# A hybrid decoder step in float32: when the down stage casts its operands, and in which order its weights

## The chip, the cores and the metric

The kernel runs on one core of one Trainium2 chip. The metric is the time of one execution in microseconds, the median of the runs shown. TensorE multiplies matrices out of SBUF into PSUM; VectorE, ScalarE and GpSimd do the element-wise work; SP issues most of the DMAs. In the profile's rows they are PE (PEld is its weight load), DVE, ACT, POOL and SP (SPq its queue).

## The reference

One layer of a decoder, for 1024 prompt tokens and 32 sampled ones (1056 in all), in float32. Attention and a state-space mixer come first; the stage of this change is the second half of the feed-forward block:

```python
def post_mixer(h, mix, p, w_out, ln1_g, ln1_b, w_up, w_down, w_pe, w_pg, b_pg, ln2_g, ln2_b):
    h1 = layer_norm(ALPHA * h + mix @ w_out, ln1_g, ln1_b)
    ff = jnp.square(jax.nn.relu(h1 @ w_up)) @ w_down
    e = jax.nn.sigmoid(h1 @ w_pg + b_pg) * (p @ w_pe)
    return layer_norm(ALPHA * h1 + ff + e, ln2_g, ln2_b)
```

`w_up` is 1024 x 4096, `w_down` 4096 x 1024.

## The kernel before

**Split numbers.** Every matmul operand is held as two tiles of the matmul type: a high part, made by a cast on ScalarE (`S.copy`), and a low part, the float32 value minus the high part. A product is then three matmuls, high x high, high x low and low x high.

**Seven products for eight.** The matrix product with `w_down` is done in 2 x 2 blocks by a Strassen-Winograd scheme: seven products per block. Four of the seven take sums of weight blocks as weights (`s1` to `s4`, made by `sums` on GpSimd: s1, then s2 from s1, s3, and s4 from s2), three take a weight block itself (high part `whi`, low part `wlo`). A sum gets its high part from ScalarE (`ring`, tile `a`) and its low part on GpSimd. The operands of the seven products were made by the up stage and lie in DRAM (`gd`).

**Groups and units.** The loop over `gr` (0 to 6, seven groups) walks over the inner dimension, the loop over `m` (0 to 3, four units) over the output columns. A unit is seven products in the order of `PO` (P1, P2, P3, P5, P7, P6, P4; products 0 to 6 in what follows), each of 12 matmuls of 128 x 264 into one PSUM tile `pd`; there are four such banks, taken in turn. Each product is evacuated into the accumulator `pacc` of its `m`: an addition on VectorE, or in group 0 for four of the seven a copy on ScalarE (L1599). Products 2, 3, 4 and 5 use the sums s4, s1, s3 and s2. The up stage runs before group 0, and an eighth group with the layer norm (the tail) after group 6. After units 0 and 1 of group 6, `combine` adds up a finished accumulator, half on VectorE and half on GpSimd; for units 2 and 3 the tail does it.

**Operands.** Seven operands per group, common to its four units, are loaded one group ahead. `put` is a generator: its first step issues the load (L1427), its second casts the high part on ScalarE and subtracts the low part on VectorE (L1429 and a subtraction in the helper at L82). Two are loaded in unit 0, two in unit 1, one in unit 2, and the last two, for products 5 and 6, in unit 3. There are 12 operand slots; a slot comes free when the last product on its old operand is done.

**Weights.** `dload` fetches the raw weights of the next unit in four DMAs (L1443), with two buffers. `split` makes `whi` and `wlo` (VectorE), `dsums` the four sums and their parts; the four `a` tiles are a ring.

**What sets the order.** A scheduler orders the instructions of each engine from the program and its own estimate of times, and may move an instruction over others; each engine then runs its own list strictly in order. `tc.issue_after(...)` holds what stands under it behind a given instruction; `newest(engine)` is the last one written so far for an engine. So a list is neither the program's order nor free of it.

Of the kernel before, what the change touches and what calls it, by code (L numbers as in the profile page):

```python
# [69 lines left out]
def fox_s5_step(tc, a, o):  # L70
    nc = tc.nc
    V, S, G, PE, SY = nc.vector, nc.scalar, nc.gpsimd, nc.tensor, nc.sync
# [8 lines left out]
    def tt(e, out, x, y, op):  # L81
        e.tensor_tensor(out, x, y, op=op)  # L82
# [27 lines left out]
    def bank2(name, tag="w"):  # L110
        return cur["pool"].tile([128, 2, 512], F32, tag=tag, name=name, bufs=cur["bufs"][tag])
# [44 lines left out]
    def split(x, hi, lo, e=V):  # L156
        S.copy(hi, x)  # L157
        tt(e, lo, x, f(hi), SUB)
# [6 lines left out]
    def newest(engine):  # L165
        return [i for i in nc.cur_bb.bb.instructions if i.engine == engine][-1]
# [136 lines left out]
    with ExitStack() as st1:  # L303
# [127 lines left out]
        for l in range(L):  # L431
            j = L - 1 - l
# [296 lines left out]
        for u in range(3):  # L729
            ps = flip()  # L730
            n = 4 if u < 2 else 1
# [550 lines left out]
    for n, i in enumerate(order):  # L1282
# [3 lines left out]
        if 0 < n < 8:  # L1286
            x = order[n + 1]
# [37 lines left out]
    with ExitStack() as st1:  # L1325
# [24 lines left out]
        for m in range(8):  # L1350
            w = load_w(a["w_pg"][0][:, 128 * m:128 * m + 128]) if m > 1 else wg[m]
            if m < 4:
                x, y = [pp.tile([128, 2, HN], F32, tag=f"x{j}", name="x") for j in range(2)]
# [33 lines left out]
    def sums(p, x11, x12, x21, x22, n):  # L1387
        s1, s2, s3, s4 = (p.tile([128, 4 if p is up_ else n, 128], F32, tag=f"s{j}", name="s")[:, 0:n] for j in range(4))
        tt(G, s1, x21, x22, ADD)
        tt(G, s2, s1, x11, SUB)  # L1390
        tt(G, s3, x11, x21, SUB)
        tt(G, s4, x12, s2, SUB)
        return s1, s2, s3, s4

    def ring(p, x, n, bufs, e=V):
        x_ = p.tile([128, 2, 4 if p is up_ else n, 128], F32R, tag="a", name="a", bufs=bufs)[:, :, 0:n]
        split(x, x_[:, 0], x_[:, 1], e)
        return x_[:, 0], x_[:, 1]
# [5 lines left out]
    def product(ps, w, x, n, start):  # L1404
        for k in range(n):
            for j, (wt, xt) in enumerate(((w[0], x[0]), (w[0], x[1]), (w[1], x[0]))):
                for p in range(2):
                    PE.matmul(ps[:, p, :PC], lhsT=wt[:, k], rhs=xt[:, k, p * PC:(p + 1) * PC],  # L1408
                              start=(start and k == 0 and j == 0), stop=(k == n - 1 and j == 2), skip_group_check=True)
# [10 lines left out]
    def xslot():  # L1420
        n = (6, 7, 0, 1, 8, 9, 2, 3, 10, 11, 4, 5)[gn[0] % 12]
        gn[0] += 1
        return dn.tile([128, 2, 2, HN], F32R, tag=f"x{n}", name="x")

    def put(gr, c):
        xx = xslot()
        SY.dma_start(out=f(xx[:, 1]), in_=gd[gr][:, c])  # L1427
        yield
        S.copy(xx[:, 0], f(xx[:, 1]))  # L1429
        tt(V, xx[:, 1], f(xx[:, 1]), f(xx[:, 0]), SUB)  # L1430
        yield xx[:, 0], xx[:, 1]
# [3 lines left out]
    def q(x, fh, dh):  # L1435
        return x.rearrange("p (f k h) c -> p f k h c", f=2, k=2)[:, fh, :, dh]

    def dload(gr, m):
        raw, hi, lo = wraw()
        for j, z in enumerate((2 * gr, 2 * gr + NP_)):  # L1440
            for dh in range(2):
                d0 = (4 * dh + m) * 128
                SY.dma_start(out=q(raw, j, dh),  # L1443
                             in_=a["w_down"][0][z * 128:z * 128 + 256, d0:d0 + 128].rearrange("(k p) c -> p k c", p=128))
        return raw, hi, lo

    def accload(m):
        for u in range(2):
            SY.dma_start(out=pacc[m][:, P2 + 2 * u:P4 + 2 * u], in_=accd[m + 4 * u].rearrange("p (a n) -> p a n", a=2))

    def dsums(p, w, bufs, ss=None):
        raw, hi, lo = w
        if ss is None:
            ss = sums(p, q(raw, 0, 0), q(raw, 1, 0), q(raw, 0, 1), q(raw, 1, 1), 2)
        s1, s2, s3, s4 = (ring(p, x, 2, bufs, G) for x in ss)
        x11, x12, x22 = ((q(hi, fh, dh), q(lo, fh, dh)) for fh, dh in ((0, 0), (1, 0), (1, 1)))
        return (P1, x11), (P2, x12), (P3, s4), (P5, s1), (P7, s3), (P6, s2), (P4, x22)

    with ExitStack() as st1:
        up_ = pool("up", stack=st1)  # L1460
        for i in range(NP_):
# [7 lines left out]
            s1, s2, s3, s4 = sums(up_, r0[:, 0:4], r0[:, 4:8], r1[:, 0:4], r1[:, 4:8], 4)  # L1469
            s2, s1, s3, s4, x22 = (ring(up_, x, 4, 5) for x in (s2, s1, s3, s4, r1[:, 4:8]))  # L1470
# [71 lines left out]
            with tc.manual_schedule(engines={mybir.EngineType.Activation, mybir.EngineType.DVE}):  # L1542
                for c in "wp4ps5p6ppppab":
                    if c == "p":
                        xs_[PO[len(xs_)]] = next(st.pop(0))
                    elif c == "w":
                        split(*w)
                        ss = sums(up_, *(q(w[0], fh, dh) for fh, dh in ((0, 0), (1, 0), (0, 1), (1, 1))), 2)
                    elif c == "s":
                        ws = dsums(up_, w, 5, ss)  # L1550
                    elif c == "a":
                        square(0)
                    elif c == "b":
                        tc.keep_in_program_order(square(1))
                    else:
                        evac(int(c))
# [9 lines left out]
    def combine(m):  # L1566
        x = pacc[m]
        for n, (o, z) in enumerate(((P6, P1), (P2, P1), (P3, P5), (P7, P6), (P3, P6), (P4, P7), (P8, P5), (P8, P7))):
            tt((V, G, G, V, V, V, G, G)[n], x[:, o], x[:, o], x[:, z], ADD)

    for gr in range(NG_ - 1):
        st = [put(gr + 1, c) for c in (range(7) if gr < NG_ - 2 else (0, 3, 1, 2))]
        nx = []
        for m in range(4):
            if gr or m:
                if gr == 0:
                    accload(m)
                split(*wn)
                ws = dsums(dw, wn, 4)
            if gr and m == 0:  # L1580
                with tc.issue_after(newest(mybir.EngineType.Activation)):
                    for j in (P6, P4):
                        xs_[j] = next(xs_[j])
            put_ = [st.pop(0) for _ in range(min((2, 2, 1, 0)[m], len(st)))]
            for x in put_:
                next(x)
            with ExitStack() as st1:
                if put_:
                    st1.enter_context(tc.issue_after(newest(mybir.EngineType.SP)))
                if gr or m:  # L1590
                    wn = dload(gr + m // 3, (m + 1) % 4)
                else:
                    wn = w1
            for n, (j, w) in enumerate(ws):
                ps = bank2("pd", "b")
                product(ps, w, xs_[j], 2, True)
                o = pacc[m][:, j].rearrange("p (a n) -> p a n", a=2)
                if gr == 0 and j < P2:
                    S.copy(o, ps[:, :, :PC])  # L1599
                else:  # L1600
                    tt(V, o, ps[:, :, :PC], o, ADD)
                if m == 3 and n < 2 and st:
                    nx.append(st.pop(0))
                    next(nx[-1])
                if n in (3, 5) and put_:
                    nx.append(next(put_.pop(0)))
            if gr == NG_ - 2 and m < 2:
                combine(m)
        xs_ = dict(zip(PO, nx)) if gr < NG_ - 2 else {1: nx[0:2], 0: nx[2:4]}
# [3 lines left out]
    for m in range(4):  # L1613
        raw, hi, lo = dload(NG_ - 1, m) if m else wn
        if m > 1:
            x = xslot().rearrange("p a k n -> p (a k n)")
# [4 lines left out]
    with ExitStack() as st1:  # L1621
# [6 lines left out]
        for c0, c1, ts_ in ((792, NT, (7, 8)), (HN, 792, (5, 6)), (256, HN, (2, 3, 4)), (0, 256, (0, 1))):  # L1628
# [15 lines left out]
            for n, m in enumerate(ms):  # L1644
                ps = bank("mml")[:, :c1 - c0]
                for fh in range(2):
                    w, x = ws[m % 4][m // 4][fh], xs_[th][fh]
# [93 lines left out]
```

## Time and profile before

| | us |
|---|---|
| median of 3 runs (1489.22 to 1490.48) | 1489.49 |
| the profiled execution | 1489.35 |
| its span, first to last instruction | 1487.6 |
| TensorE busy | 1394.8 (94%) |
| VectorE busy | 984.8 (66%) |
| GpSimd busy | 676.9 (46%) |
| ScalarE busy | 638.8 (43%) |
| down stage, first matmul on `pd` to first of the tail | 1086.70 to 1414.05 |

Busy shares are means over stages with different limits, so the stage has to be read by itself. Times in the rows are microseconds from the start of the span. A row of the windows has the stretch, its length, the busy time (and number of instructions) of PE, PEld, DVE, ACT and POOL, the granted clock of TensorE as a share of its full 2.4 GHz, the busy share of the DMA engines, and the GB/s they moved. The windows of the units are cut at the first matmul of every unit, each 84 matmuls after the last. A row of a timeline has start and length, engine, line, operation, the tile written and those read, their shapes and the number of instructions merged; in brackets the engine's idle time before it and what ended it. L82 is a helper's line, so there the tiles tell what is done: `x<-x` is the low part of an operand, `wlo` that of a weight block, `a<-s,a` that of a weight sum, `s<-` a sum, `pacc<-pd,pacc` an evacuation, `pacc<-pacc` an addition of `combine`.

### The profile page before, as it was taken

How to read it: one execution, taken by the hardware profiler on the slowest of the kernel's cores; microseconds unless marked ns; L12 is line 12 of the kernel's file. 1: busy time of each engine (PE TensorE's matmuls, PEld its weight loads, DVE VectorE, ACT ScalarE, POOL GpSimd, SP SyncE). 2: the span in 40 equal slices, each digit the busy share in tenths (PEclk: the TensorE clock that was granted, in tenths of full speed). 3: DMA queues.
4: the chain of work that ended last, by engine and by line, in shares of the span. 5: the costliest groups of instructions: out<-in, count | busy, mean ns of one | idle time of the engine just before them, and what ended most of it. 6: DMA issues, size and time to landing. Idle time of an engine off the chain costs nothing. (4 is left out here: it accounts for less than half of the span.)

```text
span 1487.6 us, 26536 instructions
## 1 busy us (share of the span) xinstructions
PE 1394.8 (94%) x10045; PEld 1274.6 (86%) x10045; DVE 984.8 (66%) x1591; ACT 638.8 (43%) x1188; POOL 676.9 (46%) x627
## 2 busy tenths in 40 slices
PE   6998999979999899999999999999989999999886
PEld 5787898977757657799999999999989999899886
DVE  8559599558867644678745555555366667777777
ACT  4423434446756523452324444444475324344112
POOL 4313011126666400048655334443267667676935
PEclk8999999989999999999999999999999999999998
DMA  7564355596765582232234443444394423444212
GB/s 274 180 128 103 96 145 148 176 245 162 188 175 143 164 244 61 77 90 81 91 100 160 159 145 120 140 153 160 110 349 145 144 89 101 159 151 140 69 35 99
DMA packets 205736, 211.89 MB, mean 142 GB/s; under 512 B 43592, under 2 KB 166088, under 8 KB 205608
## 3 DMA queue, kind: packets, MB, share of 16 engines
q1 hardware_dynamic: 197288, 178.02, 41.4%
q0 software_dynamic: 8320, 32.18, 5.6%
q8 instruction: 79, 1.29, 0.3%
q14 instruction: 49, 0.40, 0.1%
HBM read 143.59 MB, written 66.55 MB: 141 GB/s over the span
## 5 line engine op out<-in xcount | busy, mean ns | idle before, releaser
L1408 PE MATMUL pd<-x,a 128*128 128x264 f32 x1344 | 176.0, 289 | 19.4 <-POOL a L82 12.5
L1408 PEld LDWEIGHTS pd<-x,a 128*128 128x128 f32 x1344 | 169.9, 192 | 22.8 <-POOL a L82 14.2
L82 DVE TENSOR_TENSOR pacc<-pd,pacc 128x528 f32<-128x528 f32 x180 | 124.3, 701 | 79.9 <-PE pd L1408 78.7
L157 ACT CAST a<-s 128x256 fp32r<-128x256 f32 (+1 forms) x176 | 83.7, 483 | 189.8 <-PE pd L1408 109.1
L82 POOL TENSOR_TENSOR a<-s,a 128x256 fp32r<-128x256 f32 x112 | 114.2, 1025 | 92.4 <-ACT a L157 92.4
L1408 PE MATMUL pb<-th,a 128*128 128x264 f32 x768 | 132.3, 284 | 0.0
L82 POOL TENSOR_TENSOR pl<-pe,ph 128x512 fp32r<-128x512 f32 (+1 forms) x96 | 100.5, 1056 | 67.8 <-DVE ph L905 43.8
L82 DVE TENSOR_TENSOR wlo<-raw,whi 128x1024 fp32r<-128x1024 f32 x68 | 100.5, 1477 | 43.6 <-ACT whi L157 30.1
L1408 PE MATMUL pd<-x,whi 128*128 128x264 f32 x672 | 111.4, 288 | 9.0 <-DVE pacc L82 6.9
L82 POOL TENSOR_TENSOR s<-raw 128x256 f32<-128x256 f32 (+1 forms) x72 | 76.9, 1071 | 75.7 <-DVE a L82 64.1
L1408 PEld LDWEIGHTS pb<-th,a 128*128 128x128 f32 x768 | 109.2, 189 | 0.0
L1408 PEld LDWEIGHTS pd<-x,whi 128*128 128x128 f32 x672 | 95.0, 191 | 10.8 <-ACT a L157 5.8
L82 DVE TENSOR_TENSOR x<-x 128x1056 fp32r<-128x1056 f32 (+2 forms) x67 | 89.3, 1349 | 13.1 <-ACT x L1429 12.5
L183 PE MATMUL mmc<-hhi,whi 128*128 128x352 f32 x288 | 94.6, 329 | 0.0
L183 PE MATMUL mmc<-hhi,wlo 128*128 128x352 f32 x288 | 94.3, 328 | 0.0
L183 PE MATMUL mmc<-hlo,whi 128*128 128x352 f32 x288 | 93.8, 326 | 0.0
L82 POOL TENSOR_TENSOR rs<-rs,mh 128x1 f32<-128x1 f32 (+1 forms) x27 | 20.6, 770 | 160.1 <-DVE rs L86 157.8
L82 DVE TENSOR_TENSOR a<-s,a 128x512 fp32r<-128x512 f32 x64 | 48.1, 756 | 47.5 <-ACT a L157 43.3
L1408 PE MATMUL pb<-tl,a 128*128 128x264 f32 x384 | 78.0, 285 | 0.0
L157 ACT CAST whi<-raw 128x1024 fp32r<-128x1024 f32 x48 | 50.4, 1051 | 61.5 <-PE pa L1408 27.0
L882 ACT ACTIVATE row<-ss,nm 128x384 f32<-128x384 f32 (+4 forms) x96 | 55.6, 584 | 37.9 <-DVE nm L878 36.5
L1408 PE MATMUL pd<-x,wlo 128*128 128x264 f32 x336 | 69.2, 288 | 0.0
(471 smaller groups left out, 3948.4 us busy)
## 6 DMA issues: line engine op xcount, KB each, us to landing
x<-gd SPq DMA_DIRECT2D x53, 528.0 KB
raw<-in_w_up_dram SPq DMA_DIRECT2D x32, 512.0 KB
raw<-in_w_down_dram SPq DMA_DIRECT2D x128, 128.0 KB
gd<-e POOLq DMA_DIRECT2D x14, 1056.0 KB, 7.4
gd<-c POOLq DMA_DIRECT2D x14, 792.0 KB, 5.3
pg<-in_cache_k_dram SPq DMA_DIRECT2D x32, 256.0 KB
pg<-in_cache_v_dram SPq DMA_DIRECT2D x32, 256.0 KB
raw<-in_w_in_dram SPq DMA_DIRECT2D x12, 512.0 KB
```

The lines of the kernel that those rows point to most:

```text
L82: e.tensor_tensor(out, x, y, op=op)
L157: S.copy(hi, x)
L183: PE.matmul(out, lhsT=wt[:, k], rhs=xt[:, k, c0:c0 + n], start=(k == 0 and i == 0), stop=(k == nk - 1 and i == 2))
L882: S.activation(out=pr_[:, c * n:(c + 1) * n], in_=ps, func=AF.Exp, scale=-1.0, bias=nm[:, i:i + 1], accum_out=lsum[:, h, i + 4 * c:i + 4 * ...
L1408: PE.matmul(ps[:, p, :PC], lhsT=wt[:, k], rhs=xt[:, k, p * PC:(p + 1) * PC], start=(start and k == 0 and j == 0), stop=(k == n - 1 and j = ...
```

## The change

Two things are written in another order, and no instruction is added or taken out. First, `dsums` casts the sums in the order in which the products use them: s4, s1, s3, s2 (before: s1 to s4). Second, an operand that is loaded in unit m is cast in unit m + 1, right behind the weight casts of that unit (`due`, under `tc.issue_after` of the newest instruction on ScalarE). Before, its cast was written into unit m, after products 3 and 5, where nothing held it. For the last two operands of a group nothing changes in the code: they were cast behind the weight casts of unit 0 already.

```diff
         raw, hi, lo = w
         if ss is None:
             ss = sums(p, q(raw, 0, 0), q(raw, 1, 0), q(raw, 0, 1), q(raw, 1, 1), 2)
-        s1, s2, s3, s4 = (ring(p, x, 2, bufs, G) for x in ss)
+        s4, s1, s3, s2 = (ring(p, ss[j], 2, bufs, G) for j in (3, 0, 2, 1))
...
-        nx = []
+        nx, due = [], []
         for m in range(4):
...
                     for j in (P6, P4):
                         xs_[j] = next(xs_[j])
+            for x in due:
+                with tc.issue_after(newest(mybir.EngineType.Activation)):
+                    nx.append(next(x))
             put_ = [st.pop(0) for _ in range(min((2, 2, 1, 0)[m], len(st)))]
             for x in put_:
                 next(x)
+            due = put_[:]
...
-                if n in (3, 5) and put_:
-                    nx.append(next(put_.pop(0)))
```

How this moves the engines' lists is seen at three places. SP's list stays as it was. The lists of units 0 to 3 of groups 1 to 5 repeat.

The first place is the change from group 1 to group 2. ScalarE, before: `x_13313` and `x_13329` are the operands of products 5 and 6 of group 2, the other `x` belong to group 3; `a_13417` and `a_13420` are weights of unit 0, `whi_13432` and `a_13550` on those of unit 1.

```order
L157 CAST a_13417<-s_13405 128x256
L1429 CAST x_13427<-x_13427 128x1056
L157 CAST a_13420<-s_13406 128x256
L1429 CAST x_13313<-x_13313 128x1056
L1429 CAST x_13329<-x_13329 128x1056
L1429 CAST x_13429<-x_13429 128x1056
L157 CAST whi_13432<-raw_13431 128x1024
L1429 CAST x_13562<-x_13562 128x1056
L1429 CAST x_13564<-x_13564 128x1056
L157 CAST a_13550<-s_13542 128x256
L157 CAST a_13553<-s_13543 128x256
L1429 CAST x_13697<-x_13697 128x1056
```

Now, at the same place (`s_13406` is s4, `s_13403` s1; the weights of unit 1 are `a_13546` to `a_13555`):

```order
L157 CAST a_13411<-s_13406 128x256
L157 CAST a_13414<-s_13403 128x256
L157 CAST a_13417<-s_13405 128x256
L157 CAST a_13420<-s_13404 128x256
L1429 CAST x_13313<-x_13313 128x1056
L1429 CAST x_13329<-x_13329 128x1056
L157 CAST whi_13432<-raw_13431 128x1024
L157 CAST a_13546<-s_13541 128x256
L157 CAST a_13549<-s_13538 128x256
L157 CAST a_13552<-s_13540 128x256
L157 CAST a_13555<-s_13539 128x256
L1429 CAST x_13427<-x_13427 128x1056
```

All seven operand casts stood among the weight casts of two units; now two stand behind the four weight casts of each unit, in unit 3 one.

VectorE at the same place, before (`pd_13387` is the last product of group 1, `pd_13438` to `pd_13466` products 0 to 2 of unit 0):

```order
L82 TENSOR_TENSOR x_13427<-x_13427 128x1056
L82 TENSOR_TENSOR pacc3_12354<-pd_13387,pacc3_12354 128x528
L82 TENSOR_TENSOR x_13313<-x_13313 128x1056
L82 TENSOR_TENSOR x_13329<-x_13329 128x1056
L82 TENSOR_TENSOR pacc0_12249<-pd_13438,pacc0_12249 128x528
L82 TENSOR_TENSOR x_13429<-x_13429 128x1056
L82 TENSOR_TENSOR pacc0_12249<-pd_13452,pacc0_12249 128x528
L82 TENSOR_TENSOR wlo_13433<-raw_13431,whi_13432 128x1024
L82 TENSOR_TENSOR x_13562<-x_13562 128x1056
L82 TENSOR_TENSOR pacc0_12249<-pd_13466,pacc0_12249 128x528
L82 TENSOR_TENSOR x_13564<-x_13564 128x1056
```

Now:

```order
L82 TENSOR_TENSOR pacc3_12354<-pd_13387,pacc3_12354 128x528
L82 TENSOR_TENSOR x_13313<-x_13313 128x1056
L82 TENSOR_TENSOR x_13329<-x_13329 128x1056
L82 TENSOR_TENSOR pacc0_12249<-pd_13438,pacc0_12249 128x528
L82 TENSOR_TENSOR wlo_13433<-raw_13431,whi_13432 128x1024
L82 TENSOR_TENSOR pacc0_12249<-pd_13452,pacc0_12249 128x528
L82 TENSOR_TENSOR pacc0_12249<-pd_13466,pacc0_12249 128x528
L82 TENSOR_TENSOR pacc0_12249<-pd_13480,pacc0_12249 128x528
L82 TENSOR_TENSOR pacc0_12249<-pd_13494,pacc0_12249 128x528
L82 TENSOR_TENSOR pacc0_12249<-pd_13508,pacc0_12249 128x528
L82 TENSOR_TENSOR pacc0_12249<-pd_13522,pacc0_12249 128x528
L82 TENSOR_TENSOR x_13427<-x_13427 128x1056
```

The operand parts that stood between the evacuations of products 0 to 4 have gone to the ends of units 0, 1 and 2.

The second place is ScalarE at the end of unit 0 of group 0, before. `c4_12037` is the last output of the up stage, which SP writes to DRAM; `pd_12402`, `pd_12418` and `pd_12432` are products 3 to 5.

```order
L1475 ACTIVATE c4_12037<-c4_12037 128x1056
L1476 ACTIVATE c4_12037<-c4_12037 128x528
L1429 CAST x_12356<-x_12356 128x1056
L1475 ACTIVATE c4_12037<-c4_12037 128x528
L1599 COPY pacc0_12249<-pd_12402 128x528
L1429 CAST x_12358<-x_12358 128x1056
L1599 COPY pacc0_12249<-pd_12418 128x528
L1429 CAST x_12486<-x_12486 128x1056
L1599 COPY pacc0_12249<-pd_12432 128x528
L1429 CAST x_12488<-x_12488 128x1056
L157 CAST whi_12491<-raw_12490 128x1024
L1429 CAST x_12623<-x_12623 128x1056
```

Now (`pd_12497` is product 0 of unit 1, and the `a` are the four weights of unit 1):

```order
L1475 ACTIVATE c4_12037<-c4_12037 128x1056
L1476 ACTIVATE c4_12037<-c4_12037 128x528
L1475 ACTIVATE c4_12037<-c4_12037 128x528
L1603 COPY pacc0_12249<-pd_12402 128x528
L1603 COPY pacc0_12249<-pd_12416 128x528
L1603 COPY pacc0_12249<-pd_12430 128x528
L157 CAST whi_12491<-raw_12490 128x1024
L1603 COPY pacc1_12355<-pd_12497 128x528
L157 CAST a_12470<-s_12465 128x256
L157 CAST a_12473<-s_12462 128x256
L157 CAST a_12476<-s_12464 128x256
L157 CAST a_12479<-s_12463 128x256
```

Five operand casts have left this stretch; in both lists the weight casts of unit 1 come behind the copy of its product 0.

The third place is GpSimd in group 6, before: the low parts of the weights of unit 26 (unit 2 of group 6; `a_15854` is s4's), among sums for the next unit and the additions of `combine` for `pacc1`.

```order
L82 TENSOR_TENSOR s_15964<-raw_15857 128x256
L82 TENSOR_TENSOR a_15848<-s_15838,a_15848 128x256
L82 TENSOR_TENSOR a_15851<-s_15839,a_15851 128x256
L82 TENSOR_TENSOR pacc1_12355<-pacc1_12355 128x528 x2
L82 TENSOR_TENSOR a_15854<-s_15840,a_15854 128x256
```

Now (`a_15841` is s4's, `a_15850` s2's):

```order
L82 TENSOR_TENSOR a_15841<-s_15836,a_15841 128x256
L82 TENSOR_TENSOR a_15844<-s_15833,a_15844 128x256
L82 TENSOR_TENSOR a_15847<-s_15835,a_15847 128x256
L82 TENSOR_TENSOR pacc1_12355<-pacc1_12355 128x528
L82 TENSOR_TENSOR s_15964<-raw_15857 128x256
L82 TENSOR_TENSOR pacc1_12355<-pacc1_12355 128x528 x2
L82 TENSOR_TENSOR s_15966<-raw_15857 128x256
L82 TENSOR_TENSOR a_15850<-s_15834,a_15850 128x256
```

The last of the four low parts is s2's now, for product 5, and no longer s4's, for product 2.

## Rows read from the trace of the kernel before

**Rows 1.** Windows by unit: units 0 to 3 of group 2.

```profile
1183.11:1195.41 12.30, 10.62 (x86) 10.26 (x85) 12.30 (x13) 8.76 (x13) 11.37 (x8) 1.00 0.75 250
1195.41:1207.02 11.61, 10.59 (x84) 10.39 (x85) 8.10 (x11) 2.44 (x6) 10.81 (x13) 1.00 0.16 47
1207.02:1217.24 10.22, 10.22 (x86) 10.22 (x85) 6.09 (x8) 2.68 (x6) 5.78 (x9) 1.00 0.00 0
1217.24:1227.46 10.22, 10.22 (x86) 10.22 (x85) 6.09 (x8) 2.73 (x5) 3.13 (x5) 1.00 0.70 220
```

**Rows 2.** Windows by group: 0, 1 to 5, 6, and the tail.

```profile
1086.70:1135.78 49.08, 42.86 (x339) 42.44 (x338) 25.40 (x25) 29.52 (x49) 31.96 (x34) 0.97 0.73 256
1135.78:1362.83 227.05, 211.63 (x1683) 208.39 (x1682) 163.50 (x195) 87.72 (x137) 157.10 (x160) 0.98 0.41 131
1362.83:1414.03 51.20, 44.51 (x338) 42.93 (x337) 42.09 (x47) 15.62 (x25) 48.34 (x39) 0.97 0.33 103
1414.03:1487.60 73.57, 56.91 (x458) 54.71 (x456) 57.05 (x109) 12.47 (x17) 33.94 (x28) 0.94 0.18 67
```

**Rows 3.** Window of the up stage.

```profile
768.00:1086.00 318.00, 318.00 (x2616) 318.00 (x2616) 167.94 (x218) 151.25 (x236) 133.52 (x110) 1.00 0.43 146
```

**Rows 4.** Timeline of TensorE at four places: start, length, work, [idle before it, releaser].

```profile
1106.50 7.51 PE L1408 MATMUL pd<-x,a 128*128 128x264 f32 x48 [4.87 <-ACT a L157]
...
1186.03 6.00 PE L1408 MATMUL pd<-x,a 128*128 128x264 f32 x48
...
1193.63 0.72 PE L1408 MATMUL pd<-x,whi 128*128 128x264 f32 x4 [1.59 <-DVE pacc L82]
...
1398.29 3.56 PE L1408 MATMUL pd<-x,a 128*128 128x264 f32 x20 [2.47 <-POOL a L82]
```

**Rows 5.** Timeline of VectorE in unit 0 of group 2.

```profile
1191.08 1.79 DVE L82 TENSOR_TENSOR x<-x 128x1056 fp32r<-128x1056 f32 x1
...
1192.79 0.69 DVE L82 TENSOR_TENSOR pacc<-pd,pacc 128x528 f32<-128x528 f32 x1
```

**Rows 6.** Waits of TensorE from 1086 to the end: total, times, longest.

```profile
PE pd L1408 <- POOL a L82: 12.5, 8, 2.5
PE pd L1408 <- DVE pacc L82: 8.4, 6, 1.8
```

**Rows 7.** Timeline of ScalarE in unit 0 of group 2.

```profile
1193.21 1.07 ACT L1429 CAST x<-x 128x1056 fp32r<-128x1056 f32 x1 [2.76 <-DMA x<-gd]
```

**Rows 8.** Window behind the wait in unit 1 of group 0.

```profile
1106.60:1109.60 3.00, 3.00 (x14) 3.00 (x15) 0.00 (x0) 0.00 (x0) 3.00 (x6) 0.50 1.02 408
```

**Rows 9.** Groups of VectorE's instructions, 1132 to 1362: busy, mean ns | idle before.

```profile
L82 DVE TENSOR_TENSOR pacc<-pd,pacc 128x528 f32<-128x528 f32 x140 | 97.2, 702 | 57.5 <-PE pd L1408 57.5
...
L82 DVE TENSOR_TENSOR x<-x 128x1056 fp32r<-128x1056 f32 x35 | 47.7, 1373 | 8.9 <-ACT x L1429 8.9
...
L82 DVE TENSOR_TENSOR wlo<-raw,whi 128x1024 fp32r<-128x1024 f32 x20 | 25.0, 1248 | 1.3
```

**Rows 10.** Timeline of GpSimd in unit 0 of group 1.

```profile
1138.37 1.64 POOL L82 TENSOR_TENSOR s<-raw 128x256 f32<-128x256 f32 x1 [3.59 <-DMA raw<-in_w_down_dram]
```

**Rows 11.** GpSimd's low parts: units 2 and 3 of group 2, then unit 0.

```profile
L82 POOL TENSOR_TENSOR a<-s,a 128x256 fp32r<-128x256 f32 x8 | 5.9, 738 | 9.6 <-ACT a L157 9.6
...
L82 POOL TENSOR_TENSOR a<-s,a 128x256 fp32r<-128x256 f32 x3 | 5.1, 1700 | 1.6 <-ACT a L157 1.6
```

**Rows 12.** Timeline of ScalarE in group 0.

```profile
1094.83 1.06 ACT L1429 CAST x<-x 128x1056 fp32r<-128x1056 f32 x1
...
1104.51 0.71 ACT L157 CAST a<-s 128x256 fp32r<-128x256 f32 x2 [0.95 <-DMA gd<-c]
```

**Rows 13.** Timeline of SP's queue in group 0.

```profile
1096.46 0.57 SPq L1512 DMA_DIRECT2D gd<-c  x1
```

**Rows 14.** Timeline of GpSimd in group 6.

```profile
1397.05 1.19 POOL L82 TENSOR_TENSOR a<-s,a 128x256 fp32r<-128x256 f32 x1
...
1408.47 0.74 POOL L82 TENSOR_TENSOR a<-s,a 128x256 fp32r<-128x256 f32 x1
```

## The prediction

> **What bounds the kernel now.** I read the windows by group first, then those by unit, then who ended TensorE's waits, and last the engines at the waits.
>
> A unit is 84 matmuls on 7 products. Undisturbed, TensorE is busy through the whole unit, which takes 10.22 us at a granted clock of 1.00, as units 2 and 3 of group 2 do [rows 1]. That is 0.1217 us a matmul and 1.46 us a product. The down stage has 28 units, so 286.2 us would do; it takes 49.08 + 227.05 + 51.20 = 327.3 us [rows 2]. So 41.2 us are lost: 8.2 in group 0, 227.05 - 204.4 = 22.65 in groups 1 to 5, and 10.3 in group 6. That the full pace can be held is seen in the up stage: 318 us with TensorE busy throughout at clock 1.00 [rows 3].
>
> In groups 1 to 5 the loss is in units 0 and 1 alone: 12.30 and 11.61 us in group 2 against twice 10.22 [rows 1]. In unit 0 VectorE is busy 12.30 of 12.30 us, and in units 2 and 3 6.09 of 10.22: the work of one group lies in a heap at its start. TensorE waits 1.59 us there for VectorE [rows 4]. It waits for a PSUM bank: product 6 takes the bank of product 2, whose evacuation at 1192.79 stood behind an operand's low part of 1.79 us [rows 5]. The wait early in unit 1 is for a weight's low part on GpSimd; over the stage GpSimd ends most of TensorE's waits and VectorE most of the others [rows 6]. ScalarE gives the reason: it waits 2.76 us for the last operand's DMA, and the weight casts of unit 1 stand behind [rows 7].
>
> A wait has a second price. After the 4.87 us in group 0, 48 matmuls took 7.51 us, where 48 take 6.00 at full pace [rows 4]: right behind the wait the granted clock is 0.50, 1.2 of 2.4 GHz, over 14 matmuls [rows 8].
>
> **The change part by part.** Nothing is added or removed: the same casts, subtractions and DMAs, and the DMA queue keeps its order. Three things move, and I cost them by where TensorE waits.
>
> *Groups 1 to 5.* Before, the five or six operand casts that the scheduler could pull forward stand around the start of unit 0, and their low parts stand between VectorE's evacuations. After, at most two stand in a unit, behind its four weight casts. VectorE's load becomes 7 evacuations at 0.702, one low weight part at 1.248 and two operand low parts at 1.373 [rows 9]: 4.9 + 1.25 + 2.75 = 8.9 us of 10.22, in every unit. GpSimd has 157.1 us in these groups [rows 2], 7.9 a unit.
>
> Inside a unit, from its start at 0: ScalarE's last weight cast comes when product 5 of the unit before ends (-1.46), the two operand casts of 1.07 [rows 7] end by +1.2. VectorE evacuates the last product by 0.8, has the operand parts by 3.5, evacuates product 0 by 4.2, does the low weights by 5.5, evacuates product 1 by 6.2 and product 2 by 6.9. Their banks are wanted at 5.84, 7.30 and 8.76. All are free in time; the smallest slack is 1.1 us. The low operand parts for products 5 and 6 of unit 0 are there at 3.5, wanted from 7.30. The weights of unit 1 land latest: GpSimd's wait for them ended at 1138.37 [rows 10], 2.6 us into group 1. From there three sums and a fourth, at up to 1.70 each [rows 11], a cast and a low part take 9 us: +11.6, wanted at 10.22 + 2.92 = 13.1; and s4, the first product's weight, is now cast first, not last. So I find no wait and take the whole 22.65 us. Bounds: 0, if other waits come in its place, and 22.65.
>
> *Group 0.* The weight casts of unit 1 need a buffer out of which a DMA still writes the up stage's last output: a cast waited for it until 1104.51 [rows 12]. That DMA was issued at 1096.46 [rows 13], behind an operand cast of 1.06 on ScalarE [rows 12] that is now elsewhere. So it lands some 1.0 earlier, 1103.5. Unit 0 saves 0.6 (a wait for s4's low part goes, one of 1.0 for a bank comes). Unit 1 then starts at 1098.0, does products 0 and 1 and 4 matmuls on the first weight cast until 1101.4, waits until 1103.9, and does 56 more: 1110.8, and half of the 1.5 of low clock, 1111.5. Before it ended at 1115.33. In unit 2 the copies out of PSUM are behind GpSimd's sums and cost about 0.9 again. Gain 2.9; bounds 0 and 8.2.
>
> *Group 6.* GpSimd is busy 48.34 of 51.20 us [rows 2], since it also adds up finished accumulators; it stays the limit. Its order holds as many instructions ahead of the last low part of unit 2 as before, which ended at 1397.05 + 1.19 = 1398.24, and TensorE started 0.05 later [rows 4, 14]. But before it was s4's, and 32 matmuls of the unit came after it; now it is s2's, and 20 come. The same for unit 3, whose last low part ends at 1408.47 + 0.74 = 1409.2 [rows 14]: then 20 matmuls, 2.4 us, end the stage at 1411.6 in place of 1414.03. Gain 2.4; bounds 0 and 10.3.
>
> *The tail* of 73.57 us [rows 2] starts from the stage's end and keeps its order: 0, within 1 us either way.
>
> Sum: 22.65 + 2.9 + 2.4 = 27.95. The profiled execution took 1489.35 us with a span of 1487.6; 0.14 under the median of 1489.49. 1489.35 - 27.95 = 1461.4.
>
> One thing speaks against the change: it brings operand low parts to units 1 and 2, where GpSimd had run freely. A 128x256 instruction of GpSimd takes 0.74 us in units 2 and 3 and 1.70 in unit 0, where VectorE is full [rows 11]. The Trainium skill, page "SBUF — State Buffer", section "Who interferes with whom", gives a reason: a VectorE instruction with two inputs in SBUF and a GpSimd instruction that reads SBUF exclude each other, and the later one blocks until the other is done. The two durations agree with it. By that rule each of the three such VectorE instructions of a unit can hold up one of GpSimd's; as the total of them is the same, it leaves the sum as it is, and it is the reason behind the third rival.
>
> **The rivals.**
> 1. *All waits go, in groups 0 and 6 too.* Then 41.2 us are saved: 1448. For it: none of the lost time is matmul work. Against it: the landing at 1103.5 and GpSimd's 48.34 us don't depend on the order of casts.
> 2. *A bank wait comes at each unit's start.* Evacuations now stand behind two operand parts and a weight part in a row. If all three run as the 1.79 of [rows 5], product 1's bank comes 2 x 0.42 + 0.54 = 1.4 later than above, and TensorE waits 0.3; if ScalarE's casts are late too by half a microsecond, 0.8. At 0.5 a unit in 20 units that is 10 us: 1471. For it: slack of 1.1. Against: the mean is 1.373 over 35.
> 3. *GpSimd becomes the bound, and the kernel is slower.* If all 8 of its instructions of a unit took 1.70, a unit would take 13.6 us, five groups 272 in place of 227.05: 1489.35 + 45 - 5.3 = 1529. It turns from gain to loss (groups 0 and 6 left out) where a unit takes 227.05 / 20 = 11.35, with (11.35 - 8 x 0.74) / 0.96 = 5.7 of 8 held up. Against: VectorE's work of this kind is 1.25 + 2.75 = 4.0 us a unit, time for two or three: 5.9 + 3 x 0.96 = 8.8.
> 4. *Nothing comes of it*, since what TensorE waits for only changes its name: within 0.2% of before. Against: VectorE's heap is what the rows show, and the new order takes it apart.
>
> **How the numbers follow.** Forecast 0.62, with a range of its own from 1455 to 1467 (groups 0 and 6 give nothing, or 12 together). Rival 1 and its neighbourhood under 1455: 0.12. Rival 2, 1467 to 1478: 0.17. Rival 4: 0.04. Rival 3: 0.04. The rest, 0.01, lies between 1478 and 1486. Less than 0.2% (3 us) is about what a measurement of this kernel cannot tell from no change. Faster 0.92, same 0.04, slower 0.04. The range 1452 to 1476 leaves out most of rival 1, a part of rival 2, and rivals 3 and 4: about 2 in 10.
>
> **What the profile would show.** Right: units of 10.2 us throughout groups 1 to 5, VectorE about 8.2 us in each and nowhere full; no wait of TensorE for the bank of product 2 in unit 0, none for a weight's low part in unit 1; clock 1.00 in these groups; the casts of unit 1 in group 0 still behind the DMA; group 6 still with GpSimd busy throughout, about 48.8 us long. Wrong: waits for VectorE at product 4 or 5 of a unit (rival 2), GpSimd busy near 10 us a unit (rival 3), or a tail that grows by what the stage gives.

## The result, and the profile after

The changed kernel took 1465.36 us (median of 4 runs, 1463.83 to 1465.46), beside 1489.36 for the kernel before: a ratio of 0.9837, 95% interval 0.9817 to 0.9856. Measured again (first experiment below) it took 1468.62 beside 1488.95, 0.9857 (0.984 to 0.9873). The saving is 24.0 us in one comparison, 20.3 in the other.

Windows by group, cut as in [rows 2], after:

```profile
1082.19:1131.56 49.37, 44.28 (x338) 43.64 (x337) 27.59 (x25) 29.65 (x51) 36.54 (x35) 0.93 0.73 257
1131.56:1336.23 204.67, 204.66 (x1683) 204.47 (x1682) 165.90 (x195) 85.18 (x136) 153.14 (x161) 1.00 0.45 145
1336.23:1389.73 53.50, 43.44 (x339) 42.52 (x337) 45.16 (x47) 15.32 (x24) 47.68 (x39) 0.97 0.32 98
1389.73:1463.70 73.97, 58.21 (x456) 56.23 (x456) 57.21 (x109) 11.43 (x16) 33.04 (x27) 0.92 0.18 67
```

Against [rows 2], groups 1 to 5 fell by 22.38 us, group 0 and the tail grew by 0.3 and 0.4, and group 6 grew by 2.3. And the stage begins at 1082.19, not 1086.70: 4.5 us came from ahead of it, where the instruction lists are the same but for the order of four weight casts at its end. The units of group 2, to be held against [rows 1]:

```profile
1172.71:1182.93 10.22, 10.22 (x87) 10.22 (x86) 8.14 (x10) 4.43 (x8) 6.89 (x9) 1.00 0.85 282
1182.93:1193.15 10.22, 10.22 (x87) 10.22 (x86) 8.72 (x10) 4.43 (x8) 9.31 (x10) 1.00 0.27 78
1193.15:1203.37 10.22, 10.22 (x87) 10.22 (x86) 8.72 (x10) 4.53 (x8) 8.96 (x10) 1.00 0.00 0
1203.37:1213.59 10.22, 10.22 (x87) 10.22 (x86) 7.53 (x9) 3.55 (x7) 5.45 (x7) 1.00 0.70 213
```

VectorE's 12.30 us in unit 0 have become 8.14, 8.72, 8.72 and 7.53 in the four units, and every unit takes 10.22. What TensorE still waits for in the stage and at the tail's first matmul (total, times, longest), against [rows 6]:

```profile
PE pd L1408 <- DVE pacc L82: 10.1, 5, 4.8
PE pd L1408 <- ACT a L157: 4.0, 2, 2.7
PE mml L1652 <- ACT whi L157: 1.0, 1, 1.0
```

All of it lies in groups 0 and 6. GpSimd's low parts have left the list; VectorE's evacuations have taken the place. The last line is the tail's first matmul, which waits for a cast of the tail's weights. Group 6 is cut at that matmul, so 1.0 of the 2.3 us by which it grew is this wait.

### The profile page after: what moved, and what is told of

The parts are those of the page before. It is cut to its first block, busy times and chain, and to the rows that moved or that the text cites. A ratio compares the mean times of both kernels' runs of the same rounds, so it can differ in the third digit from the quotient of the medians.

```text
span 1463.7 us, 26623 instructions
## 1 busy us (share of the span) xinstructions
PE 1385.4 (95%) x10045; PEld 1269.7 (87%) x10045; DVE 993.2 (68%) x1591; ACT 634.2 (43%) x1188; POOL 675.1 (46%) x627
## 5 line engine op out<-in xcount | busy, mean ns | idle before, releaser
L82 POOL TENSOR_TENSOR a<-s,a 128x256 fp32r<-128x256 f32 x112 | 99.3, 892 | 60.4 <-ACT a L157 60.2
L82 POOL TENSOR_TENSOR s<-raw 128x256 f32<-128x256 f32 (+1 forms) x72 | 72.1, 1006 | 87.6 <-DVE a L82 64.0
L82 DVE TENSOR_TENSOR x<-x 128x1056 fp32r<-128x1056 f32 (+2 forms) x67 | 94.4, 1439 | 2.5 <-ACT x L1429 1.9
```

## The experiments

Every profile was cut at the first matmul of each group and of the tail, so group 6 ends with any wait of the tail's first matmul: none in both profiles of before, e3, e7, e8, e10 and e11, 0.9 to 1.3 us in both of after, e2, e4, e6 and e9, and 2.4 in e12. Ahead of the stage no kernel does other work.

| kernel | stage begins | group 0 | 1 to 5 | 6 | tail | median | ratio to before (95%) |
|---|---|---|---|---|---|---|---|
| before | 1086.70 | 49.1 | 227.1 | 51.2 | 73.5 | 1489.36 | |
| before again | 1080.94 | 50.2 | 226.5 | 51.6 | 74.5 | 1485.63 (1 run) | |
| after | 1082.19 | 49.4 | 204.7 | 53.5 | 73.9 | 1465.36 | 0.9837 (0.9817 to 0.9856) |
| after again | 1085.54 | 48.7 | 205.3 | 54.3 | 74.1 | 1468.62 | 0.9857 (0.984 to 0.9873) |
| e2 casts later, old weight order | 1083.41 | 50.6 | 205.6 | 55.9 | 72.1 | 1468.99 | 0.9851 (0.9826 to 0.9877) |
| e3 weight order alone | 1084.25 | 48.7 | 219.2 | 51.3 | 73.9 | 1479.34 | 0.9923 (0.9907 to 0.994) |
| e4 heap in unit 3 | 1083.12 | 49.2 | 215.0 | 55.7 | 73.4 | 1478.82 | 0.9925 (0.9905 to 0.9944) |
| e6 other place in SBUF | 1081.89 | 47.8 | 204.4 | 54.0 | 74.3 | 1464.95 | 0.9832 (0.9816 to 0.9848) |
| e7 group 6 as before | 1084.83 | 49.2 | 205.9 | 50.8 | 74.4 | 1464.81 | 0.9834 (0.9818 to 0.985) |
| e8 group 6 later still | 1082.88 | 49.1 | 205.2 | 49.4 | 76.7 | 1464.99 | 0.9841 (0.9825 to 0.9856) |
| e9 no VectorE additions | 1087.87 | 49.1 | 204.4 | 49.9 | 74.2 | 1467.21 (1 run) | |
| e10 no GpSimd additions | 1085.10 | 48.4 | 205.7 | 45.2 | 74.1 | 1460.45 (1 run) | |
| e11 later loads | 1084.69 | 45.4 | 205.7 | 52.5 | 73.5 | 1460.95 | 0.9813 (0.9796 to 0.983) |
| e12 e6, e7 and e11 | 1086.76 | 44.1 | 206.3 | 53.7 | 72.3 | 1458.46 | 0.9791 (0.9767 to 0.9816) |

**How much lies ahead of the stage.** Before and after, each profiled once more with nothing edited.

> The kernel before, unchanged, with a profile of its own. The down stage began at 1086.70 us in the first profile of before and at 1082.19 in that of after, although both have the same instruction lists ahead of it. Theory (the part ahead of the stage varies from one execution to the next): the stage begins more than 1.5 us away from 1086.7, and the stage itself repeats within 1 us: 49.1, 227.0 and 51.2 us for groups 0, 1 to 5 and 6. Rival (the 4.5 us belong to the two programs): it begins within 1 us of 1086.7.

> The changed kernel, unchanged, with a second profile. In the first profile of after the down stage began 4.5 us earlier than in the first of before; the second profile of before began 5.8 us earlier too. Theory (the part ahead of the stage varies from one execution to the next, and nothing of it belongs to the change): the stage begins anywhere from 1080 to 1088 us, the stage and the tail repeat within 1 us (49.4, 204.7, 53.5 and 73.9), and over five rounds the time is 1464 to 1471. Rival (the change makes what lies ahead of the stage shorter): it begins within 1 us of 1082.2 and the time stays within 1 us of 1465.4.

Both theories held, but for group 0 of before, which repeats within 1.2 us and not within 1. Over 14 profiles the stage begins anywhere from 1080.94 to 1087.87 us, before and after alike, while the stretches behind, of the two kernels profiled twice, repeat within 1.2. Stage and tail together took 400.9 and 402.9 us before, 381.5 and 382.5 after: the change is worth 19.9 us there. In the profiled pair 4.5 us more lie ahead of the stage, where both do the same work; for the executions without a profile this can't be told apart.

**Which half carries groups 1 to 5.** e2 takes after and undoes the order of the weight sums; e3 takes before and changes that order alone (the diff is e2's, e3 has its reverse):

```diff
-        s4, s1, s3, s2 = (ring(p, ss[j], 2, bufs, G) for j in (3, 0, 2, 1))
+        s1, s2, s3, s4 = (ring(p, x, 2, bufs, G) for x in ss)
```

> The operand casts one unit later as in the change, but the weight sums cast in the old order s1 to s4. Theory (the gain of groups 1 to 5 is the end of VectorE's heap, so the place of the operand casts carries it): groups 1 to 5 take 205 to 215 us and the time is 1463 to 1475; what is lost against the whole change are waits at product 2 for the low part of s4, whose cast waits for the buffer that product 5 of the unit before gives back. Rival (the order of the weight casts carries it): groups 1 to 5 stay above 221 us and the time above 1482.

> The weight sums cast in the order of the products as in the change, but the operand casts where they stood before. Theory (VectorE's heap): unit 0 of each of the groups 1 to 5 still takes 12.3 to 13 us with a wait for VectorE, the waits for a low part in unit 1 go; groups 1 to 5 take 214 to 222 us, and the time is 1478 to 1486. Rival (the order of the weight casts carries the gain): 205 to 210 us, and 1464 to 1472.

The place of the operand casts alone brings groups 1 to 5 from 226.8 (mean of two) to 205.6, with one wait of 0.9 us for a low part left. TensorE's waits in these groups of e2:

```profile
PE pd L1408 <- POOL a L82: 0.9, 1, 0.9
```

The weight order alone brings 219.2: it takes away all waits for low parts, but unit 0 keeps the heap (13.1 to 13.8 us in groups 2 to 5, where 12.3 to 13 was expected, and 10.5 in group 1). Units 0 and 1 of group 2 in e3:

```profile
1175.50:1189.00 13.50, 11.10 (x87) 10.36 (x85) 12.55 (x13) 9.63 (x14) 11.45 (x8) 1.00 0.67 224
1189.00:1199.30 10.30, 10.30 (x85) 10.30 (x86) 8.12 (x11) 2.34 (x6) 9.55 (x11) 1.00 0.18 52
```

Unit 1 is healed, and unit 0, with VectorE at 12.55 us, is no better than in [rows 1]. The two halves don't add up (21.2 and 7.5 against 21.8 together), since either one heals unit 1: beyond 10.22 us a unit, groups 1 to 5 lose 13.6 us in unit 0 and 9.0 in unit 1 in the first profile of before, 13.1 and 1.7 in e3, 0.0 and 1.2 in e2.

**The heap put back elsewhere.** e4 collects the five operands until unit 3 (groups 1 to 5):

```diff
-            for x in due:
+            for x in due if m == 3 or gr in (0, NG_ - 2) else ():
...
-            due = put_[:]
+            due = put_[:] if gr in (0, NG_ - 2) else due + put_
```

> After, but in groups 1 to 5 the five operands of units 0 to 2 are all cast in unit 3, behind its weight casts; groups 0 and 6 as in after. It puts VectorE's heap back, at another place: 7 x 0.70 + 1.25 + 5 x 1.37 = 13.0 us of VectorE in a unit of 10.22. Theory (a heap on VectorE costs what the banks cannot take up): unit 3 takes 11.7 to 13 us with waits for VectorE at products 5 and 6, units 0 to 2 stay near 10.2; groups 1 to 5 take 212 to 219 us, the time is 1472 to 1480. Rival (any place behind the weight casts will do): groups 1 to 5 within 2 us of 204.7, the time 1464 to 1467.

Unit 3 now takes 11.58 us, a little under the 11.7 expected, and the unit behind it 10.9 to 11.4, where 10.2 was expected; TensorE waits for VectorE alone in these groups. Its waits there, then unit 3 of group 1:

```profile
PE pd L1408 <- DVE pacc L82: 6.5, 9, 0.9
...
1163.02:1174.60 11.58, 10.65 (x87) 10.25 (x85) 11.38 (x12) 8.51 (x12) 8.02 (x7) 1.00 0.73 233
```

VectorE is full (11.38), GpSimd is not (8.02). So it isn't enough that an operand is cast behind the weights; it is VectorE's load per unit that decides. This heap costs 10 us (215.0 against 205.0, the mean of after).

**Group 0: the DMA that unit 1 waits for.** e6 takes the accumulators from SBUF ahead of the weight sums' buffers:

```diff
-    dw = pool("downw", stack=dctx)
     pap = pool("pacc", stack=dctx)
     pacc.update({m: pap.tile([128, 8, HN], F32, name=f"pacc{m}") for m in (2, 3, 1)})
+    dw = pool("downw", stack=dctx)
```

> After, with the three accumulators taken from SBUF before the buffers of the weight sums, so that these no longer lie where SP's DMA still writes the up stage's last output from. Theory (unit 1 of group 0 waits for that DMA, and pays again in clock): ScalarE's wait for the DMA and the second wait of TensorE go, and with them most of the low clock; the wait of 1.4 us behind the weights' own DMA stays; unit 1 takes 11.5 to 13 us, group 0 44 to 46 in place of 49.4, and the time falls by 3.5 to 5.5 against after. Rival (the wait only moves, to the accumulators' loads or to the weights behind them): group 0 within 1 us of 49.4, or another unit of it longer by as much.

Half a miss: unit 1 takes 16.10 us and group 0 47.8. In after, ScalarE's list in unit 1 is:

```profile
1096.32 1.05 ACT L157 CAST whi<-raw 128x1024 fp32r<-128x1024 f32 x1 [3.24 <-DMA raw<-in_w_down_dram]
1097.28 0.59 ACT L1603 COPY pacc<-pd 128x528 f32<-128x528 f32 x1
1097.77 0.41 ACT L157 CAST a<-s 128x256 fp32r<-128x256 f32 x1
1101.17 1.01 ACT L157 CAST a<-s 128x256 fp32r<-128x256 f32 x3 [3.00 <-DMA gd<-c]
```

Two DMAs hold it: the weights of unit 2 hold the first cast that product 2 needs, the up stage's output the second. In e6 the four casts run in one go, but VectorE then evacuates product 1 only at

```profile
1101.91 0.71 DVE L82 TENSOR_TENSOR pacc<-pd,pacc 128x528 f32<-128x528 f32 x1 [4.13 <-POOL s L82]
```

The profile names GpSimd, but an evacuation reads no weight sum. It waits for the load of its accumulator too, which stands behind that output on the same queue: issued at 1091.89, it reports the last part of its landing at 1101.79, 0.12 us before VectorE starts, and the same 0.12 us lie between the two in after and in e11. TensorE waits 2.68 us for the bank, and group 0 gains 0.9 to 1.6 us only.

e11 issues the five operands of group 1 (2.6 MB at 528 KB each) behind the accumulators' loads. Until now all five stood ahead of the output and of the accumulator, and four of them ahead of the weights of unit 2:

```diff
...
-            put_ = [st.pop(0) for _ in range(min((2, 2, 1, 0)[m], len(st)))]
-            for x in put_:
-                next(x)
+            put_ = [st.pop(0) for _ in range(min((2, 2, 1, 0)[m] if gr else (0, 3, 2, 0)[m], len(st)))]
+            if gr:
+                for x in put_:
+                    next(x)
...
-                    st1.enter_context(tc.issue_after(newest(mybir.EngineType.SP)))
+                    st1.enter_context(tc.issue_after(newest(mybir.EngineType.SP) if gr else anchor[max(m - 1, 0)]))
...
+            if gr == 0:
+                for x in put_:
+                    with tc.issue_after(anchor[m]):
+                        next(x)
```

(`anchor[m]` is the last DMA of `accload(m)`.)

> After, but in group 0 the first five operands of group 1 are loaded behind the accumulators' loads of units 1 and 2 (three and two), no longer ahead of the weights of unit 2 and of the up stage's last output. Theory (the waits of unit 1 are for a busy DMA queue: the weights, that output and the accumulator each stand behind 2.6 MB of operands which nothing needs before group 1): the two waits of 1.4 and 2.7 us go, and with them the low clock; unit 1 takes 10.3 to 11.5 us, group 0 42 to 45 in place of 49, and the time falls by 4 to 7 against after. Rival (the queue was not the reason, or the operands are late now): group 0 within 1.5 us of 49, or waits in units 2 and 3 in exchange.

Unit 1 takes 11.45 us (17.36 and 15.75 in after), the clock stays at 1.00, and group 0 takes 45.4 us, 3.6 less than the mean of after. The output lands 6.5 us after its issue, in place of 10.0 and 9.3 in after. Group 0 misses 42 to 45 since unit 2 now waits once, for a copy on ScalarE behind a weight cast that itself waited 4.7 us for a sum on GpSimd, and since not all of unit 1's wait went. Group 0 of e11, its window and TensorE's waits:

```profile
1084.69:1130.12 45.43, 41.78 (x339) 41.14 (x338) 26.77 (x25) 29.79 (x51) 36.41 (x35) 1.00 0.79 279
...
PE pd L1408 <- ACT pacc L1610: 1.7, 1, 1.7
PE pd L1408 <- DVE pacc L82: 1.1, 1, 1.1
PE pd L1408 <- ACT a L157: 0.9, 1, 0.9
```

**Group 6: what makes it longer.** e7 casts the last group's operands where before did, e8 in units 2 and 3:

```diff
-            due = put_[:]
+            due = put_[:] if gr < NG_ - 2 else []
...
+                if n in (3, 5) and put_ and gr == NG_ - 2:
+                    nx.append(next(put_.pop(0)))
```

```diff
-            for x in due:
+            for x in (due if gr < NG_ - 2 else due[2 * m - 4:2 * m - 2] if m > 1 else ()):
...
-            due = put_[:]
+            due = put_[:] if gr < NG_ - 2 else due + put_
```

> After, but in group 6 the four operands of the last group are cast where they were before, in the unit that loads them. Theory (cast one unit later they fall into units 1 and 2 of that group, where the additions of combine fill VectorE): group 6 takes 50.5 to 52 us in place of 53.5, groups 1 to 5 stay at 204.7, and the time falls by 1.5 to 3 against after. Rival (the new order of the weight sums makes group 6 longer): 53 us or more, no change of the time.

> After, but in group 6 the four operands of the last group are cast later still, two in unit 2 and two in unit 3. VectorE's work in units 1, 2 and 3 is then 11.2, 13.9 and 8.9 us (7 evacuations of 0.70, a weight part of 1.25, four additions of 1.25 in units 1 and 2, two operand parts of 1.37 in units 2 and 3); now it is 13.9, 13.9 and 6.2. Theory (VectorE is the limit of these units): unit 1 falls from 14.3 to about 11.5, unit 2 stays, and group 6 takes 50 to 52 us in place of 53.5. Rival (GpSimd is the limit, with weight sums and additions): within 1 us of 53.5 or more, with TensorE's waits for a low part of a weight.

e7 brings group 6 to 50.8, below before's 51.2 and 51.6, as its theory said: the later casts cost it 2.7 to 3.5 us. With the casts at the old place the new weight order gives 0.6 (e7) or 0.1 (e3), which these profiles can't tell from nothing. e8 gives more, 49.4 (50 to 52 was expected), but the tail pays 2.7 of it back, and TensorE then waits 2.9 us for low parts on GpSimd. Which engine is it? Unit 0 has lost its heap here too (13.07 us before, 10.22 in after), so the loss lies in the units behind it, which took 11.88 and 16.04 before. Units 1 and 2 of group 6 in after:

```profile
1346.45:1360.69 14.24, 10.70 (x86) 10.33 (x85) 14.16 (x15) 3.15 (x7) 13.65 (x11) 1.00 0.05 15
1360.69:1378.35 17.66, 12.12 (x87) 11.76 (x85) 14.40 (x14) 4.64 (x9) 17.07 (x15) 0.90 0.17 49
```

Both VectorE and GpSimd are full in unit 1. e9 and e10 take away one or the other half of `combine` (e9: `e is G`, e10: `e is V`):

```diff
-            tt((V, G, G, V, V, V, G, G)[n], x[:, o], x[:, o], x[:, z], ADD)
+            e = (V, G, G, V, V, V, G, G)[n]
+            if m > 1 or e is G:
+                tt(e, x[:, o], x[:, o], x[:, z], ADD)
```

> After, without VectorE's four additions in each of the two calls of combine in group 6 (those on the finished accumulators of units 0 and 1 are left out, GpSimd's four stay; so a part of the sum is not formed). Read by the stretch of group 6 alone, 53.5 us in after. Theory (VectorE's work in units 1 and 2, 13.9 us a unit, is what delays the evacuations): 8.9 us are left, units 1 and 2 take 10.2 to 11.5 us, group 6 42 to 45. Rival (GpSimd, which makes the weight sums and does the other half of combine, is the limit): 49 us or more, with waits for a low part of a weight.

> After, without GpSimd's four additions in the same two calls of combine (VectorE's four stay; so a part of the sum is not formed). Theory (VectorE is the limit): the waits for VectorE in units 1 and 2 stay; they shrink by what GpSimd's additions held up of VectorE's (additions of 1.2 in place of 1.5 to 1.8, the wait of 1.3 for GpSimd), and group 6 takes 47 to 51 us. Rival (GpSimd is the limit): group 6 takes 42 to 45.

My theory fell. Without VectorE's additions unit 1 is healed (10.42), but units 2 and 3 wait 5.4 us for low parts on GpSimd, and group 6 still takes 49.9. Without GpSimd's it takes 45.2, nearly what the rival said. But e10 takes away three things at once, GpSimd's work, VectorE's wait of 1.3 us for one of these additions, and what they add to VectorE's times (below); their shares are not told apart. TensorE's waits in group 6 of e9:

```profile
PE pd L1408 <- POOL a L82: 5.4, 2, 3.2
```

and of e10:

```profile
PE pd L1408 <- DVE pacc L82: 3.3, 3, 1.2
```

Nor is VectorE's work the same in the two. Its groups in group 6 (count | busy, mean ns), after:

```profile
L82 DVE TENSOR_TENSOR pacc<-pd,pacc 128x528 f32<-128x528 f32 x28 | 18.8, 698 | 5.3 <-PE pd L1408 5.2
L82 DVE TENSOR_TENSOR pacc<-pacc 128x528 f32<-128x528 f32 x8 | 10.9, 1372 | 1.3 <-POOL pacc L82 1.3
L82 DVE TENSOR_TENSOR x<-x 128x1056 fp32r<-128x1056 f32 x6 | 9.6, 1615 | 0.0
```

and e10:

```profile
L82 DVE TENSOR_TENSOR pacc<-pd,pacc 128x528 f32<-128x528 f32 x28 | 18.8, 698 | 3.8 <-PE pd L1408 3.6
L82 DVE TENSOR_TENSOR pacc<-pacc 128x528 f32<-128x528 f32 x8 | 8.6, 1089 | 0.1
L82 DVE TENSOR_TENSOR x<-x 128x1056 fp32r<-128x1056 f32 x6 | 7.9, 1338 | 0.0
```

With eight of GpSimd's fourteen additions in this stretch gone, VectorE's additions take 1089 ns, not 1372, its operand parts 1338, not 1615; the evacuations, which read PSUM, stay at 698. The Trainium skill, page "SBUF — State Buffer", section "Who interferes with whom", gives a reason: VectorE with two inputs in SBUF excludes a GpSimd instruction that reads SBUF, with one it does not. The trace agrees in which instructions grow longer; that one excludes the other outright, these means do not show.

**All together.** e12 takes e11 (two operands in unit 1, three in unit 2), e6 and e7.

> Three edits on after at once: group 0's operand loads behind the accumulators' loads (two in unit 1, three in unit 2), the accumulators placed where the up stage's last output lay, and the old place of the operand casts in group 6. Theory (the three act in separate places and add up): unit 1 of group 0 near 10.3 us, group 0 42 to 45, groups 1 to 5 near 205, group 6 50.5 to 52, the tail 73.5 to 74.5, and 1455 to 1460. Rival (each wait taken away in group 0 uncovers the next one of the same DMA queue): group 0 stays at 45 or above and the time at 1459 to 1463.

The fastest version by its median: 1458.46 us, with an interval that ends just below those of both measurements of after and overlaps that of e11. Group 0 takes 44.1, though its unit 1 takes 11.47 and not 10.3. Group 6 missed, 53.7 with a tail of 72.3, and 2.4 of the 53.7 are the wait of the tail's first matmul; the two sum to 125.9, beside 127.4 and 128.4 in after and 125.2 in e7.

## Why the prediction was right, and where not

**Groups 1 to 5: right, reason and size.** Forecast 22.65, measured 22.38 (two profiles each: 21.8). Both causes that the prediction names were at work. VectorE's heap cost 13.6 us in unit 0, and it goes with the place of the operand casts (e2, e3, e4). In unit 1 the weight casts that stood behind operand casts on ScalarE cost 9.0, and either half of the change takes most of that away (e2, e3). No wait came in their place, but for 0.27 us in unit 0 of group 1 of the first profile. GpSimd was busy 153 us, 7.7 a unit and at most 9.31 in group 2, so rivals 2 to 4 fell here.

The slack that was put at 1.1 us, from the end of product 1's evacuation to the first matmul of product 5, was 0.9 to 1.1 in units 0 to 2 of the first profile of after, but for that one unit, and 0.7 to 1.2 in the second. What the schedule left out is when the next unit's weights land. In e7, e10, e11 and e12 unit 0 of group 4 took 1.0 to 1.3 us more: ScalarE waited 3.6 to 4.0 us for that DMA, and VectorE's weight part and product 1's evacuation stood behind. The wait is that of rival 2, in one unit of twenty, but not for rival 2's reason. Why the DMA came late there, I have not traced. In e12:

```profile
1259.28 1.05 ACT L157 CAST whi<-raw 128x1024 fp32r<-128x1024 f32 x1 [4.04 <-DMA raw<-in_w_down_dram]
```

Two smaller readings were off, and nothing in the sum rests on them. VectorE's 8.9 us hold for three units of four, as unit 3 casts one operand (7.53). And in the stage GpSimd ended 12.5 of TensorE's 27.5 us of waits, not most of them: VectorE ended 8.4 and ScalarE 6.6.

**Group 0: the step that failed is "So it lands some 1.0 earlier, 1103.5".** The DMA was issued earlier in the stage, by 0.8 us (1091.14, 8.95 behind the stage's start, against 9.76 [rows 13]), but landed 1.2 later: 18.98 behind the start (1101.17) against 17.81 [rows 12]. It took 10.0 us in place of 8.0. The issue in after:

```profile
1091.14 0.57 SPq L1512 DMA_DIRECT2D gd<-c  x1
```

In the second profiles it took 9.3 us in place of 9.0 and landed 0.2 earlier. The step took the DMA's time as fixed, which it is not, and the 1.0 came in neither pair; with the operands' loads behind it (e11) the DMA takes 6.5 us. One more thing was left out: the first cast stands behind a cast that waits for the weights of unit 2 (1.39 us of TensorE, 0.91 in the second profile). The term for the low clock, half of the 14 matmuls of before, can't be held against the change at all (last section). Forecast gain 2.9, measured -0.3 (two profiles each: 0.6). That the queue, not the casts, limits unit 1 is shown by e11.

**Group 6: the step that failed is "now it is s2's, and 20 come".** It took the last low part on GpSimd for what starts TensorE. The low part of s2 ended 1370.93 + 1.70 = 1372.63, 36.4 us into the group (35.4 for s4's before). But TensorE could not use it. GpSimd, VectorE and TensorE there:

```profile
1370.93 1.70 POOL L82 TENSOR_TENSOR a<-s,a 128x256 fp32r<-128x256 f32 x1
```

```profile
1368.60 1.79 DVE L82 TENSOR_TENSOR pacc<-pacc 128x528 f32<-128x528 f32 x1 [1.28 <-POOL pacc L82]
1370.31 1.74 DVE L82 TENSOR_TENSOR wlo<-raw,whi 128x1024 fp32r<-128x1024 f32 x1
1371.97 1.22 DVE L82 TENSOR_TENSOR pacc<-pacc 128x528 f32<-128x528 f32 x1
1373.12 1.31 DVE L82 TENSOR_TENSOR pacc<-pd,pacc 128x528 f32<-128x528 f32 x2
```

```profile
1373.96 2.98 PE L1408 MATMUL pd<-x,a 128*128 128x264 f32 x12 [4.79 <-DVE pacc L82]
```

The evacuation that frees the bank of product 5 stands at 1373.12, behind an addition that waited for GpSimd, a weight part and another addition. I had added up VectorE's work per unit for groups 1 to 5 (8.9 us), but not for group 6, where `combine`'s four additions come on top: 13.9 of 10.22 in two units. Forecast gain 2.4, measured -2.3 (two profiles each: -2.5), of which 1.0 and 1.3 us are the wait of the tail's first matmul. That GpSimd with its additions matters more than VectorE's additions is borne out by e9 and e10; but in after no matmul of group 6 waits for a low part, so it limits through VectorE and not, as the step had it, directly.

**The tail:** forecast 0, measured +0.4 (two profiles each: 0.0).

**The sum.** 27.95 was forecast and 19.4 came in the stage and the tail of the profiled pair. That the time lay within 4 us of the forecast owes 4.5 us to the start of the stage, which is luck: it scatters over 7 us.

## What to carry to other kernels

Add up each engine's work for each unit of the loop, not for the stage: groups 1 to 5, with VectorE busy 72% of the time (163.50 of 227.05 us), lost 4.5 us each, 2.7 of them in the one unit that had 12.3 us of VectorE's work for 10.2. Do the sum for the first and last groups separately; extra work there turns the same move into a loss. Compare the stretch that a change touches: in the profiled pair here, 4.5 us came from ahead of it.

## What was not expected of the hardware

How many matmuls run at the low clock behind a wait could not be told from the wait. After the single wait of 4.87 us in unit 1 of group 0 before, matmuls were started 0.22 us apart 12 times in a row (0.1217 at full pace), and after the single wait of 4.72 in the second profile of before 25 times. In after it was two shorter waits, 1.39 and 2.65 us, 3.4 us apart, and 24 times; in its second profile 0.91 and 2.52, and 15 times. So the first pair alone would show a price of the change that the second pair takes back. TensorE behind the wait in the second profile of before, then behind the second wait in the first of after, to be held against the 48 matmuls in 7.51 us of [rows 4]:

```profile
1100.63 8.80 PE L1408 MATMUL pd<-x,a 128*128 128x264 f32 x48 [4.72 <-ACT a L157]
```

```profile
1101.63 8.17 PE L1408 MATMUL pd<-x,a 128*128 128x264 f32 x44 [2.65 <-ACT a L157]
```

The granted clock in these stretches was 0.50, 1.2 of 2.4 GHz, as in [rows 8]. A window of the second profile of before and one of the first of after:

```profile
1100.73:1103.73 3.00, 3.00 (x14) 3.00 (x15) 0.71 (x1) 0.00 (x0) 3.00 (x6) 0.50 0.94 345
```

```profile
1101.72:1104.72 3.00, 3.00 (x14) 3.00 (x15) 2.23 (x2) 2.42 (x4) 3.00 (x4) 0.50 0.81 279
```

Undisturbed units come at two paces at a granted clock of 1.00 in both: 10.22 us in after, 10.27 all through groups 1 to 5 of its second profile:

```profile
1134.21:1339.55 205.34, 205.34 (x1683) 205.34 (x1682) 167.72 (x195) 85.16 (x136) 155.06 (x161) 1.00 0.45 144
```

In e7, e8, e11 and e12 the pace changed once, at unit 0 of group 4, in either direction. It makes 1 us over 20 units.
